# The head of a two-block transformer kernel rebuilt: dummy matmuls, squares on GpSimd, one transfer for small inputs, forget logs earlier, rotary tables later

## The chip, the cores and the metric

The kernel runs on one core of one Trainium2 chip. The metric is device microseconds from start to end of one execution; the profile's page and trace come from one profiled execution of the same program. TensorE is called PE below, VectorE DVE, ScalarE ACT, GpSimd POOL, SyncE SP.

## The reference, cut to what matters

256 tokens of width 1024 pass through two blocks of two layers each. The change touches the start of the first layer, and the place where the second block's rotary tables are made. With the shapes cut out:

```python
def rms_norm(x, g):
    y = x * lax.rsqrt(jnp.mean(x * x, axis=-1, keepdims=True) + NORM_EPS)
    return y * g

def even_layer(x, ln_g, w_in, w_out, ...):
    z = rms_norm(x, ln_g) @ w_in
    aq, ak, av, ag, bq, bk, bv, bg, bf = split_cols(z, EVEN_SPLITS)
    aq, ak = rms_norm(aq, a_qn_g), rms_norm(ak, a_kn_g)      # per head
    lam = exp(sum(a_lq1 * a_lk1)) - exp(sum(a_lq2 * a_lk2)) + lam_init
    a_out = diff_attention(aq, ak, av, lam, lam_init, a_subln_g)   # softmax - lam * softmax
    log_f = jax.nn.log_sigmoid(bf + b_f_bias)
    b_out = forgetting_attention(bq, bk, bv, log_f)          # scores + cumsum of log_f
    mixed = concat([a_out * silu(ag), b_out * silu(bg)])
    return x + mixed @ w_out

def rope_angles(positions, rot_dim):                         # used in the second block alone
    ang = positions[..., None] * ROPE_THETA ** (-arange(0, rot_dim, 2) / rot_dim)
    return cos(ang), sin(ang)
```

## The kernel before, in words

**Matmuls.** All weights lie in one array in the order in which they are used, and come in blocks of 128x1024 (`fetch`, L127, on SP's queue; `raw`). Each operand is split into a high part, which ACT writes by a copy to a rounded type (`wh`, L176, and for activations `ar`, L290), and the rest, which DVE gets by a subtraction (`wl`, L177, and `ar`, L291). Three matmuls (high by high, low by high, high by low) then stand for one. `tokens` (L200) puts tokens on the output's rows, `features` (L231) puts output columns there. A block of weights is split in two pieces of 512 columns.

**The norm of x.** The layer's input is not normalized before the matmul. The factor of each token is worked out beside it and applied to the results. For that ACT squares the four pieces of x (L323, L326), DVE adds them up (L327, `acc`) and folds the two halves (L332), PE sums over the partitions (`col_sums`, L338), and DVE makes the reciprocal square root in nine small operations (L356 and L110 to L120) and puts it into `rk` (L361).

**The head.** In program order: loads of the gains, of x in four pieces and of the first weights; the split of x; the first two projections (`first`, 96 matmuls); the sum of squares; then attention A's queries and keys, whose normalized heads (`u`, L447) are turned by PE with transposes (L399, into `tp`) before scores can be made. The forget gate is eight columns wide (`narrow`, 16 matmuls at L148): its zero padded weights `wn` are cleared by POOL (L140), filled by ACT (L142) and DVE (L143). Its logarithm needs an Exp and a Ln on ACT (L899, L901), and PE sums it over the tokens with the triangular matrix `upto` (L914), which POOL prepares in `u` (L851 to L855) and DVE casts (L857). POOL also clears 12 halves of the block-diagonal key buffers `kbh` and `kbl` (L389), builds masks (L836 to L843), copies pieces of `ident` (L848, L861), and issues the loads of five small inputs (lams, sinks, forget bias, positions, frequencies).

**Order.** Instructions of each engine stand in an order that a scheduler makes from priorities (program order, shifted by `high_priority`), and each engine works its list off in that order, with waits on the other engines. The layer's units run by a string, `ORDER0`, in which AW are attention A's scores and softmaxes, AT the transposes of its weights (L553), BL the forget log. In the page and the trace a line number can be that of a helper: names of tiles tell which use it is.

## Time and profile before

| | us |
|---|---|
| time, median of 3 runs | 864.96 |
| lowest and highest of the 3 | 863.84, 866.10 |
| the profiled execution, its own time | 868.05 |
| its span in the trace | 866.4 |
| PE busy | 840.8 (97%) |
| DVE, ACT, POOL busy | 670.6, 577.7, 40.7 |

The span is from the first to the last instruction of the core; the profiled execution's own time has 1.65 us around it, and lies 3.09 us above the median of the runs without a profile. The mean granted clock of TensorE is 0.996 of full speed. Times inside the trace are counted from the start of the span.

### The profile page before, as it was taken

The numbers are of one execution on the slowest core, as the hardware profiler recorded it, in microseconds if no ns is written. First come the engines' busy times: TensorE is split into PE (matmuls) and PEld (weight loads), VectorE is DVE, ScalarE is ACT, GpSimd is POOL, SyncE is SP. The second block draws the span as 40 slices with busy tenths as digits, with TensorE's granted clock in tenths as the row PEclk, the third lists the DMA queues.
The fourth block names the chain that finished last, engine by engine and source line by source line (L and its number), as shares of the span: only waits on it lengthen the run. The fifth ranks groups of instructions, "written<-read, shape, count | busy, mean of one in ns | idle before, by whom it ended". The sixth has DMA issues, their size and how long they took to land. (4 is left out here: it accounts for less than half of the span.)

```text
span 866.4 us, 17641 instructions
## 1 busy us (share of the span) xinstructions
PE 840.8 (97%) x6554; PEld 808.7 (93%) x6554; DVE 670.6 (77%) x1799; ACT 577.7 (67%) x1379; POOL 40.7 (5%) x90
## 2 busy tenths in 40 slices
PE   6899999999999999999999999998999999999996
PEld 6899999999999999899999999998999998899986
DVE  6779997889898789988665576678999865557654
ACT  6597985779796576976654455556997665346542
POOL 9100000001000100000000000002000000000000
PEclk9999999999999999999999999999999999999999
DMA  7544344644634632246656656543324565555651
GB/s 263 166 161 139 107 142 158 198 158 143 230 97 160 184 108 91 97 137 184 191 194 190 180 192 194 187 139 104 112 73 157 183 190 180 186 187 184 218 163 48
DMA packets 40677, 138.09 MB, mean 159 GB/s; under 512 B 4960, under 2 KB 7152, under 8 KB 40592
## 3 DMA queue, kind: packets, MB, share of 16 engines
q1 hardware_dynamic: 39456, 134.20, 47.9%
q0 software_dynamic: 848, 2.25, 0.9%
q8 instruction: 51, 0.84, 0.4%
q10 hardware_dynamic: 288, 0.52, 0.2%
q14 instruction: 34, 0.28, 0.1%
HBM read 135.91 MB, written 1.05 MB: 158 GB/s over the span
## 5 line engine op out<-in xcount | busy, mean ns | idle before, releaser
L176 ACT ACTIVATE wh<-raw 128x512 fp32r<-128x512 f32 (+2 forms) x548 | 289.8, 570 | 202.8 <-issue 103.2
L177 DVE TENSOR_TENSOR wl<-raw,wh 128x512 fp32r<-128x512 f32 (+2 forms) x548 | 322.4, 618 | 115.6 <-ACT wh L176 111.9
L231 PE MATMUL mm<-ar,wh 128*128 128x256 f32 (+1 forms) x1664 | 301.0, 281 | 0.5 <-ACT ar L714 0.5
L231 PEld LDWEIGHTS mm<-ar,wh 128*128 128x128 f32 (+1 forms) x1664 | 255.0, 188 | 2.0 <-ACT ar L714 1.3
L200 PE MATMUL mm<-wh,ar 128*128 128x256 f32 (+2 forms) x1168 | 237.4, 299 | 8.1 <-ACT wh L176 6.6
L231 PE MATMUL mm<-ar,wl 128*128 128x256 f32 x832 | 232.8, 281 | 0.0
L200 PEld LDWEIGHTS mm<-wh,ar 128*128 128x128 f32 x1168 | 187.9, 192 | 13.4 <-ACT wh L176 6.7
L200 PE MATMUL mm<-wl,ar 128*128 128x256 f32 (+2 forms) x584 | 173.9, 298 | 1.1 <-DVE wl L177 1.1
L231 PEld LDWEIGHTS mm<-ar,wl 128*128 128x128 f32 x832 | 155.9, 188 | 0.3 <-DVE wl L177 0.2
L200 PEld LDWEIGHTS mm<-wl,ar 128*128 128x128 f32 x584 | 111.7, 191 | 4.3 <-DVE wl L177 1.9
L231 PE MATMUL s<-ar,wh 128*128 128x256 f32 x512 | 90.4, 279 | 0.0
L231 PEld LDWEIGHTS s<-ar,wh 128*128 128x128 f32 x512 | 77.9, 188 | 0.0
L231 PE MATMUL s<-ar,wl 128*128 128x256 f32 x256 | 71.4, 279 | 0.0
L537 ACT ACTIVATE se<-sx,mx 128x256 f32<-128x256 f32 (+1 forms) x128 | 57.2, 452 | 4.8 <-DVE mx L534 4.3
L231 PEld LDWEIGHTS s<-ar,wl 128*128 128x128 f32 x256 | 48.1, 188 | 0.0
L231 PE MATMUL pv<-ar,wh 128*128 128x256 f32 x256 | 45.1, 279 | 0.0
L231 PEld LDWEIGHTS pv<-ar,wh 128*128 128x128 f32 x256 | 39.0, 188 | 0.0
L231 PE MATMUL pv<-ar,wl 128*128 128x256 f32 x128 | 35.7, 279 | 0.0
L557 DVE TENSOR_TENSOR pt<-tp,pt 128x384 fp32r<-128x384 f32 x60 | 32.2, 552 | 3.5 <-ACT pt L556 2.8
L506 PE MATMUL s<-kbh,ar 128*128 128x512 f32 (+1 forms) x112 | 31.2, 355 | 0.5 <-ACT kbh L410 0.4
L556 ACT ACTIVATE pt<-tp 128x384 fp32r<-128x384 f32 x60 | 27.9, 486 | 1.1 <-PE tp L555 0.7
L1217 ACT ACTIVATE ar<-u 128x512 fp32r<-128x512 f32 x32 | 20.3, 633 | 11.7 <-DVE u L1215 11.7
(307 smaller groups left out, 1145.8 us busy)
## 6 DMA issues: line engine op xcount, KB each, us to landing
raw<-in_weights SPq DMA_DIRECT2D x242, 512.0 KB, 3.6
bias<-in_alibi SPq DMA_DIRECT2D x12, 192.0 KB, 2.8
bias<-in_relpos POOLq DMA_DIRECT2D x8, 192.0 KB, 2.8
raw<-in_weights SPq DMA_DIRECT2D x4, 384.0 KB, 2.8
xT<-in_x SPq DMA_DIRECT2D x4, 256.0 KB, 4.8
raw<-in_weights SPq DMA_DIRECT2D x4, 192.0 KB, 2.3
raw<-in_weights SPq DMA_DIRECT2D x2, 256.0 KB, 4.4
ar<-in_final_norm POOLq DMA_DIRECT2D x2, 256.0 KB, 5.2
```

The costliest lines, as they stand in the source:

```text
L176: nc.scalar.activation(hi[:, c:e], raw[:, c:e], AF.Copy)
L177: nc.vector.tensor_tensor(out=lo[:, c:e], in0=raw[:, c:e], in1=hi[:, c:e].bitcast(F32), op=OP.subtract)
L200: nc.tensor.matmul(view[t], lhsT=x[:, s], rhs=w[:, j, :], start=(k + j == 0 and i == 0 and (t == 0 or not one)), stop=(k + j == nkt - 1 an ...
L231: nc.tensor.matmul(acc[:width, m * T:(m + 1) * T], lhsT=w[:, j, m * P:m * P + width], rhs=x, start=(k + j == 0 and i == 0 and m == 0), sto ...
L506: nc.tensor.matmul(o, lhsT=a_[:, gq, qt * P:(qt + 1) * P], rhs=b_[:, gk, 0:n], start=(i == 0), stop=(i == 2 and last))
L537: nc.scalar.activation(e[:, c:c + n], x[:, c:c + n], AF.Exp, bias=m[:, i:i + 1], scale=-1.0, accum_out=z[:, i:i + 1])
L556: nc.scalar.activation(h, p[:, :W], AF.Copy)
L557: nc.vector.tensor_tensor(out=l, in0=p[:, :W], in1=h.bitcast(F32), op=OP.subtract)
L1217: nc.scalar.activation(h, u, AF.Copy)
```

## The change

What it does, part by part:

- **Loads.** The gains lie in front of x in one array `xg`; the first piece of x brings them along (128x576). The second piece of x is issued by ACT's queue, the rest by SP's. The five small inputs come as one array `small` (128x298), loaded once on SP's queue into a temporary, and its first 26 columns once more for the rotary tables.
- **Dummy matmuls.** 18 matmuls of 128x128 on a tile of ones (L282 of the changed kernel) stand ahead of everything on PE.
- **Squares on POOL.** All four squares of x and the three adds are TENSOR_TENSOR instructions of GpSimd on 128x512; DVE keeps the fold of the halves (now L342).
- **POOL's list.** The masks come first; the clearing of `kbh` and `kbl` goes far back; the copies of pieces of `ident` go to DVE; four loads leave its queue.
- **Forget logs.** `narrow`, the log and its split are made before attention A's keys are split and before its values; only the sum over tokens (`forget_sum`) stays as the unit BL, after AW1 instead of after AW0.
- **Rotary tables.** The load that they need moves behind the first layer's work on POOL's queue, and with it the whole computation.

The diff at its core:

```diff
-ORDER0 = ("AW0 BL AW1 BV0 AT0 AQ1 AT1 BQ0 ...
+ORDER0 = ("AW0 AW1 BL BV0 AT0 AQ1 AT1 BQ0 ...
...
-        nc.gpsimd.memset(w.bitcast(F32), 0.0)
+        with self.tc.high_priority(offset=500):
+            nc.gpsimd.memset(w.bitcast(F32), 0.0)
...
+    load_x(0, nc.sync)
+    load_x(1, nc.scalar)
+    N.fetch(flat("even_w_in"), 0, 2, 0, 256)
+    N.fetch(flat("even_w_in"), 2, 2, 0, 256, into=N.fetched[:, 512:])
+    load_x(2, nc.sync)
+    load_x(3, nc.sync)
     warm = keep.tile([P, 1], F32, name="warm")
     nc.scalar.activation(warm, ones2[:, 0:1], AF.Exp)
...
+    with tc.high_priority(offset=2000):
+        one, idle = N.arena(F32)[:, :P], N.ps("tp")
+        nc.vector.memset(one, 1.0)
+        for _ in range(WARM):
+            nc.tensor.matmul(idle[:, :P], lhsT=one, rhs=one, start=True, stop=True)
...
+              with tc.high_priority(offset=-300 - 50 * i):
                 nc.gpsimd.memset(z[rw].rearrange("p n (t e c) -> p (n t) e c", t=2, e=2)[:, :, e, :].bitcast(F32), 0.0)
...
     for dp in range(4):
-        squares(dp, st)
+        squares(dp, st, idle=True)
...
+    small = N.tmp("rx", S_COLS)
+    nc.sync.dma_start(out=small, in_=a["small"])
...
-    diff_qk(0)
-    diff_split(0)
-    diff_v(0)
+    with tc.high_priority(offset=300):
+        diff_qk(0)
...
-    nc.gpsimd.memset(both, 0.0)
+    nc.vector.memset(both, 0.0)
     for c in (0, 32):
-        nc.gpsimd.tensor_copy(both[c:c + 32, :], ident[c:c + 32, c:c + 32])
+        nc.vector.tensor_copy(both[c:c + 32, :], ident[c:c + 32, c:c + 32])
...
-        nc.gpsimd.tensor_copy(mine[c:c + 32, :], ident[c:c + 32, c:c + 8])
+        nc.vector.tensor_copy(mine[c:c + 32, :], ident[c:c + 32, c:c + 8])
...
+        return lf4
+
+    def forget_sum():
+        lf4 = gb["f"]
...
+    gb["f"] = forget_log()
+    diff_v(0)
+    diff_split(0)
     U = {"AQ": diff_qk, "AS": diff_split, "AV": diff_v, "AW": diff_weights, "AT": diff_turn, "AO": diff_out, "AN": diff_norm,
-         "BL": forget_log, "BQ": forget_qk, "BS": forget_split, "BV": forget_v, "BW": forget_weights,
+         "BL": forget_sum, "BQ": forget_qk, "BS": forget_split, "BV": forget_v, "BW": forget_weights,
...
-    pos_i = keep.tile([P, 2], I32, name="pos_i")
-    nc.gpsimd.dma_start(out=pos_i, in_=a["positions_2"].rearrange("b (t p) -> p (b t)", p=P))
+    small = N.tmp("gm", T)
+    nc.gpsimd.dma_start(out=small[:, :S_SINK], in_=a["small"][:, :S_SINK])
     pos = keep.tile([P, 2], F32, name="pos")
-    nc.vector.tensor_copy(pos, pos_i)
+    nc.vector.tensor_copy(pos, small[:, S_POS:S_POS + 2].bitcast(I32))
```

Both kernels have the branch of `squares` that `idle=True` takes; before, nothing called it:

```python
            sq = N.tmp("sq") if dp else state["acc"]
            nc.gpsimd.tensor_tensor(out=sq, in0=xf, in1=xf, op=OP.mult)
            if dp:
                nc.gpsimd.tensor_tensor(out=state["acc"], in0=state["acc"], in1=sq, op=OP.add)
```

Where instructions stand now. POOL's list in the changed kernel from its sixth instruction on (`xg` holds x, L325 are the squares, L327 the adds):

```order
L868 MEMSET cmask 128x384
L872 MEMSET tri 128x384
L275 AFFINE_SELECT ident<-ident 128x128
L325 TENSOR_TENSOR acc_276<-xg 128x512
L325 TENSOR_TENSOR sq_278<-xg 128x512
L325 TENSOR_TENSOR sq_281<-xg 128x512
L327 TENSOR_TENSOR acc_276<-acc_276,sq_278 128x512
L327 TENSOR_TENSOR acc_276<-acc_276,sq_281 128x512
L325 TENSOR_TENSOR sq_284<-xg 128x512
L873 AFFINE_SELECT tri<-tri 128x256
L143 MEMSET wn_390 128x1024
L327 TENSOR_TENSOR acc_276<-acc_276,sq_284 128x512
```

Before, 12 clearings of `kbh` and `kbl` (L389) stood there, and no TENSOR_TENSOR. Those 12 clearings now come after the last add, and ahead of the last pieces of the triangular matrix, here `u_374`. POOL further down in the changed kernel:

```order
L400 MEMSET kbl_145 64x4x128 x2
L400 MEMSET kbh_142 64x4x128
L883 MEMSET u_374 128x512
L400 MEMSET kbh_142 64x4x128
L885 AFFINE_SELECT u_374<-u_374 128x128 x2
L887 MEMSET u_374 128x128
```

DVE before, from the first split of x to the fold of the halves (L332): the adds stand between the splits of x (L291) and of the weights (L177), and wait for ACT's squares.

```order
L291 SCALAR_TENSOR_TENSOR ar_94<-xT,gain,ar_93 128x256 x2
L177 TENSOR_TENSOR wl_131<-raw_78,wh_130 128x512
L327 TENSOR_TENSOR acc_257<-acc_257,sq_259 128x512
L291 SCALAR_TENSOR_TENSOR ar_100<-xT,gain,ar_99 128x256 x2
L291 SCALAR_TENSOR_TENSOR ar_106<-xT,gain,ar_105 128x256 x2
L327 TENSOR_TENSOR acc_257<-acc_257,sq_262 128x512
L177 TENSOR_TENSOR wl_163<-raw_160,wh_162 128x512 x2
L327 TENSOR_TENSOR acc_257<-acc_257,sq_265 128x512
L177 TENSOR_TENSOR wl_196<-raw_193,wh_195 128x512 x2
L177 TENSOR_TENSOR wl_228<-raw_225,wh_227 128x512 x2
L332 TENSOR_TENSOR acc_257<-acc_257 128x256
```

DVE in the changed kernel, from the same place to the first operation on PE's column sums (`st_v`); `rx_315` is the small inputs' tile, `wn_390` the forget gate's weights:

```order
L880 COPY both<-ident 32x32 x2
L180 TENSOR_TENSOR wl_182<-raw_179,wh_181 128x512 x2
L893 COPY mine<-ident 32x8 x4
L180 TENSOR_TENSOR wl_215<-raw_212,wh_214 128x512 x2
L180 TENSOR_TENSOR wl_247<-raw_244,wh_246 128x512 x2
L342 TENSOR_TENSOR acc_276<-acc_276 128x256
L802 TENSOR_SCALAR nsink<-rx_315 128x8
L449 TENSOR_REDUCE ms_332<-sq_335 128x8
L146 TENSOR_TENSOR wn_390<-raw_388,wn_390 128x8x8
L180 TENSOR_TENSOR wl_439<-raw_436,wh_438 128x512 x2
L180 TENSOR_TENSOR wl_471<-raw_468,wh_470 128x512 x2
L366 TENSOR_SCALAR st_v_288<-tp_289 128x2
```

The adds are gone from DVE's list, and the fold of the halves (L342) now waits for POOL's last add, with everything below it behind it. Further down on DVE the cast of `upto` (L889, it waits for POOL's `u_374`) stands ahead of the normalized heads (L458) that PE's transposes wait for, as it did before (L857, there some 30 instructions ahead):

```order
L122 SCALAR_TENSOR_TENSOR rs_y_295<-rs_a_296,rs_y_295 128x2
L889 CAST upto<-u_374 128x512
L116 SCALAR_TENSOR_TENSOR rs_a_346<-rs_y_345,ms_332 128x16
L180 TENSOR_TENSOR wl_687<-raw_684,wh_686 128x512
L122 SCALAR_TENSOR_TENSOR rs_y_345<-rs_a_346,rs_y_345 128x16
L458 TENSOR_TENSOR u_333<-u_333,rs_y_345 128x512
L458 TENSOR_TENSOR u_339<-u_339,rs_y_345 128x512
```

On PE the changed kernel has 96 matmuls, the column sums (L348), the 16 narrow ones (L151), 14 matmuls, two that turn the forget gate's rows (L703), 37 matmuls, and then the first transposes of the heads (L410); before it had 96, the column sums, 48, the 16 narrow ones, one, and the transposes (L399).

## Rows read from the trace of the kernel before

**Rows 1.** The page: busy us, share of the span, instructions of each engine.
```profile
PE 840.8 (97%) x6554; PEld 808.7 (93%) x6554; DVE 670.6 (77%) x1799; ACT 577.7 (67%) x1379; POOL 40.7 (5%) x90
```

**Rows 2.** Windows (start:end, length; busy us and instructions of each engine; clock, DMA).
```profile
0.00:6.56 6.56, 0.00 (x1) 0.00 (x1) 1.56 (x10) 2.97 (x6) 5.56 (x15) 1.00 0.55 170
6.56:21.45 14.89, 14.89 (x96) 14.25 (x97) 13.05 (x24) 11.27 (x23) 14.45 (x26) 1.00 0.84 303
...
29.70:33.43 3.73, 0.02 (x1) 0.00 (x1) 3.73 (x22) 1.09 (x2) 0.00 (x0) 1.00 0.58 213
33.43:48.56 15.13, 13.86 (x96) 13.38 (x97) 12.15 (x41) 10.62 (x27) 0.00 (x0) 0.89 0.35 119
48.56:866.40 817.84, 803.82 (x6295) 773.00 (x6293) 634.65 (x1677) 547.11 (x1313) 17.07 (x40) 1.00 0.49 157
```

**Rows 3.** Waits of PE (us in total, times, longest).
```profile
PE mm L200 <- ACT wh L176: 6.6, 1, 6.6
PE tp L399 <- DVE u L447: 3.9, 2, 3.7
PE tp L914 <- ACT ar L909: 1.3, 1, 1.3
```

**Rows 4.** PE's timeline (start, us, operation, count).
```profile
12.06 0.63 PE L200 MATMUL mm<-wh,ar 128*128 128x256 f32 x2
...
12.70 0.63 PE L200 MATMUL mm<-wh,ar 128*128 128x256 f32 x2
...
13.29 0.40 PE L200 MATMUL mm<-wh,ar 128*128 128x256 f32 x2
...
13.64 0.40 PE L200 MATMUL mm<-wh,ar 128*128 128x256 f32 x2
```

**Rows 5.** PE alone behind its two waits (window, length; busy; clock, DMA).
```profile
33.43:38.00 4.57, 4.57 (x26) 0.63 0.49 160
...
47.63:50.00 2.37, 2.37 (x20) 1.00 0.18 41
```

**Rows 6.** DVE's timeline in the head.
```profile
9.79 1.69 DVE L291 SCALAR_TENSOR_TENSOR ar<-xT,gain,ar 128x256 fp32r<-128x256 f32 x4
...
13.82 2.49 DVE L177 TENSOR_TENSOR wl<-raw,wh 128x512 fp32r<-128x512 f32 x4
16.22 0.41 DVE L332 TENSOR_TENSOR acc<-acc 128x256 f32<-128x256 f32 x1
...
25.05 0.15 DVE L356 TENSOR_SCALAR st_v<-tp 128x2 f32<-128x2 f32 x1
...
32.69 1.28 DVE L447 TENSOR_TENSOR u<-u,rs_y 128x512 f32<-128x512 f32 x2
```

**Rows 7.** POOL's four copies at L861: shortest, median, longest in ns.
```profile
L861 POOL COPY mine<-ident x4: 313/356/5512, 10.0 to 11.2; 32x8 f32<-32x8 f32 x4
```

**Rows 8.** POOL's groups by shape (count, busy us, mean ns).
```profile
L389 POOL MEMSET kbh<- 64x512 f32 x6 | 3.1, 518 | 0.5 <-POOLq L1496 0.3
L140 POOL MEMSET wn<- 128x1024 f32 x2 | 1.9, 952 | 283.9 <-PE pv L231 283.9
L1423 POOL TENSOR_TENSOR o<-o,ar 128x256 f32<-128x256 f32 x2 | 1.5, 732 | 47.8 <-ACT sq L1422 47.8
L853 POOL TENSOR_SCALAR_AFFINE_SELECT u<-u 128x128 f32<-128x128 f32 x2 | 0.6, 316 | 0.1
```

**Rows 9.** DVE beside POOL's L1423, which ran from 854.44 to 855.18.
```profile
854.91 0.29 DVE L114 SCALAR_TENSOR_TENSOR rs_a<-rs_y,fv 128x1 f32<-128x1 f32 x1
...
855.62 0.16 DVE L117 SCALAR_TENSOR_TENSOR rs_a<-rs_y,fv 128x1 f32<-128x1 f32 x1
```

**Rows 10.** ACT's timeline: first work on x, a table load, the last gate.
```profile
5.08 0.91 ACT L290 ACTIVATE ar<-xT,gain 128x256 fp32r<-128x256 f32 x2 [2.78 <-DMA xT<-in_x]
...
47.71 1.28 ACT L537 ACT_TABLE_LOAD   x1
...
143.05 1.16 ACT L176 ACTIVATE wh<-raw 128x512 fp32r<-128x512 f32 x2 [1.12 <-issue]
144.12 0.61 ACT L714 ACTIVATE ar<-u 128x512 fp32r<-128x512 f32 x1
```

More of the change, by code (lines that the diff above doesn't have):

```diff
@@ L251, in forward, with load_x @@
     nc.vector.memset(ones2, 1.0)
+    xg = keep.tile([P, G_PAD + KT * T], F32, name="xg")
+    gain = xg[:, :G_PAD]
+    xT = xg[:, G_PAD:].rearrange("p (k t) -> p k t", t=T)
+    def load_x(dp, queue):
+        c = slice(G_PAD + 2 * dp * T if dp else 0, G_PAD + (2 * dp + 2) * T)
+        queue.dma_start(out=xg[:, c], in_=a["x"][:, c])
+    load_x(0, nc.sync)
[4 more added lines that the diff above has]
+    load_x(3, nc.sync)
     warm = keep.tile([P, 1], F32, name="warm")
     nc.scalar.activation(warm, ones2[:, 0:1], AF.Exp)
-    gain = keep.tile([P, 64], F32, name="gain")
-    nc.sync.dma_start(out=gain[:, :G_ROWS], in_=a["gains"])
-    xT = keep.tile([P, KT, T], F32, name="xT")
-    xr = a["x"]
-    def load_x(dp):
-        nc.sync.dma_start(out=xT[:, 2 * dp:2 * dp + 2, :], in_=xr[:, 2 * dp:2 * dp + 2, :])
-    load_x(0)
-    N.fetch(flat("even_w_in"), 0, 2, 0, 256)
-    load_x(1)
-    N.fetch(flat("even_w_in"), 2, 2, 0, 256, into=N.fetched[:, 512:])
-    load_x(2)
-    load_x(3)
     ident = keep.tile([P, P], F32, name="ident")
@@ L771, in forward @@
     nc.vector.tensor_scalar(sub8, gain[:, G_SUB:G_SUB + 1], 0.8, None, op0=OP.mult)
+    small = N.tmp("rx", S_COLS)
+    nc.sync.dma_start(out=small, in_=a["small"])
+    lam4 = small[:, S_LAM:S_COLS].rearrange("p (i f) -> p i f", i=4)
+    ls = N.tiny("ls", 2)
+    lsc = N.tiny("lsc", 64)
+    for i in range(2):
+        nc.vector.scalar_tensor_tensor(out=lsc, in0=lam4[:, 2 * i, :], scalar=1.0, in1=lam4[:, 2 * i + 1, :],
+                                       op0=OP.mult, op1=OP.mult, accum_out=ls[:, i:i + 1])
+    le = N.tiny("le", 2)
+    nc.scalar.activation(le, ls, AF.Exp)
+    nlam = keep.tile([P, 1], F32, name="nlam")
+    nc.vector.scalar_tensor_tensor(out=nlam, in0=le[:, 0:1], scalar=-1.0, in1=le[:, 1:2], op0=OP.mult, op1=OP.add)
+    nc.vector.tensor_scalar(nlam, nlam, -0.2, None, op0=OP.add)
+    sink = keep.tile([P, 8], F32, name="sink")
+    nsink = keep.tile([P, 8], F32, name="nsink")
+    nc.vector.tensor_copy(sink, small[:, S_SINK:S_SINK + 8])
+    nc.vector.tensor_scalar(nsink, small[:, S_SINK:S_SINK + 8], -1.0, None, op0=OP.mult)
+    fbias = keep.tile([P, 8], F32, name="fbias")
+    nc.vector.tensor_copy(fbias, small[:, S_FORGET:S_FORGET + 8])
     U = {}
@@ L1041, in gate @@
         gates(w, (768, 1024, 2816, 3072)[i], R["fm"], osb[i], mixed, 2 * i)
-    pos_i = keep.tile([P, 2], I32, name="pos_i")
-    nc.gpsimd.dma_start(out=pos_i, in_=a["positions_2"].rearrange("b (t p) -> p (b t)", p=P))
+    small = N.tmp("gm", T)
+    nc.gpsimd.dma_start(out=small[:, :S_SINK], in_=a["small"][:, :S_SINK])
     pos = keep.tile([P, 2], F32, name="pos")
-    nc.vector.tensor_copy(pos, pos_i)
-    invf = keep.tile([P, 24], F32, name="invf")
-    nc.gpsimd.dma_start(out=invf, in_=bass.AP(tensor=a["inv_freq"].tensor, offset=a["inv_freq"].offset,
-                                              ap=[[0, P], [1, 24]]))
+    nc.vector.tensor_copy(pos, small[:, S_POS:S_POS + 2].bitcast(I32))
+    invf = small[:, S_FREQ:S_SINK]
     NA = 24
```

43 lines of the change are left out of this document (13 added, 30 removed).

## The prediction, as put on record before the changed kernel ran

> **What bounds the kernel now.** The page comes first: PE is busy 97% of the span [rows 1], so a gain can only come from the 25.6 us in which it is not, or from a faster PE. The windows put nearly half of that in the head: PE does nothing until 6.56, is busy without a gap to 29.70, stands still to 33.43, and has another 1.27 idle by 48.56; behind 48.56 it loses 14.0 in 817.8 us [rows 2]. The waits name the three: the first weights' high parts (6.6), the normalized heads `u` (3.7) and the forget logs' split (1.3) [rows 3]. PE's timeline shows a fourth loss inside busy time: three matmuls take 0.64 us at first (12.06 to 12.70) and 0.35 from 13.29 on [rows 4], half the clock against the full one; and behind the wait for `u` the clock is 0.63 for 4.57 us, which costs 4.57 x 0.37 = 1.7. Behind the wait of 1.27 it stays at 1.00 [rows 5]. So the question is where the first softmax transposes come (48.56 before). The same 213 matmuls and 16 narrow ones stand ahead of them in both kernels, and from about 126 us on PE's order is the same; what they gain or lose there is the kernel's.
>
> **The change part by part.**
>
> *Loads.* x's first piece is issued behind one other DMA now, and ACT's first work on it starts at 5.08 [rows 10]. One issue earlier, but with the gains in it and a second queue beside it: 4.5 to 5.1, I take 4.8.
>
> *Dummy matmuls.* They fill PE's idle 6.6 us and may save the half clock of the first 30 matmuls, 30 x (0.213 - 0.117) = 2.9 us [rows 4]. But PE then only reaches its next wait earlier: what ends that wait is on DVE. I count 0.
>
> *Squares on GpSimd.* The trace has no POOL TENSOR_TENSOR of 128x512. The nearest is 128x256 at 0.73 [rows 8]: twice that less the 0.1 of a smallest memset is 1.36, less the 0.31 of POOL's smallest copy [rows 7] 1.15, and without a fixed part 1.46. Seven of them at 1.36 are 9.5 us (8.0 to 10.2). Alone that is hidden: 4.8 + 9.5 + the masks' 0.45 + some waiting for x's pieces ends near 16.5, when DVE folds the halves now (16.22 + 0.41) [rows 6]. The question is whether POOL runs beside DVE. Of POOL's four copies at L861 one took 5.51 us instead of 0.31 to 0.36 [rows 7]; it ran from 11.18 to 16.69, and DVE's row of two-input operations ended at 16.63. In the other direction DVE's L114, with both inputs in SBUF, took 0.29 instead of 0.16 and ended at 855.20, as POOL's TENSOR_TENSOR ended at 855.18, while operations with one input passed it [rows 9]. So the two exclude each other when both read SBUF, and the stretch is a serial sum. DVE's share until the fold: 8 splits of x at 0.42 and 8 of the weights at 0.60 [rows 6], with a small product of 0.25 8.4. Then 4.8 + 9.5 + 0.45 + 8.4 + 0.41 = 23.6 for the end of the fold; POOL's three memsets between (0.95 for `wn` [rows 8], two small ones) can run beside DVE, or add up to 1.2. I take 24.3, against 16.63 before.
>
> The Trainium skill, SBUF — State Buffer, section Who interferes with whom, says the same in general: a VectorE instruction with two SBUF inputs contends with a GpSimd instruction that reads SBUF, and whoever issues first holds the shared port pair for the whole instruction. By that rule the two would alternate; by the row of 5.51 GpSimd waited through the whole run of VectorE's instructions. The sum of both is 24.3 either way, but alternating also delays the weights' low parts, the third case below.
>
> *From the fold to the norm's factor.* Behind the fold DVE has one product (0.25), four copies (0.4), a reduction (0.6), two small ones, `wn` (0.15) and four weight splits (2.4) before it reads the column sums: 4.0, so `st_v` at 28.3 instead of 25.05 [rows 6]. There the old list had waited for two DMAs; that wait goes with the loads on POOL's queue, and 3.2 us of lateness come in its stead.
>
> *POOL's tail.* Behind its last add (23.9) POOL has the clearings that were moved back: 12 of `kbh` and `kbl` at 0.555 apart (6.7) [rows 8], an affine select (0.3), memsets for the forget logs, `fq` and `fk` (0.59 + 0.65), two of `pt` (0.34), then `u`'s memset and selects (0.54 + 0.59 + 0.2): 9.9, so `upto`'s source is ready at 33.8. DVE comes to that cast after four more weight splits, a reduction and 14 small ones, 28.3 + 4.4 = 32.7, and waits 1.1. Behind the cast stand 12 small operations (1.0), two weight splits (1.2) and the first head (0.6): 33.8 + 0.4 + 2.8 = 37.0 for the transposes, 33.43 before: **+3.6**. PE has its 16 narrow and 51 matmuls meanwhile; with `wn` at about 26 they end by 34.5 at full clock.
>
> *Behind the transposes.* Before, 15.13 us lay between them and the softmax transposes [rows 2]. Three things come off. The forget logs' wait, 1.27: the logs are made ahead of the values, and BL's matmuls stand later. Of the matmuls some 0.6 us moved ahead of the transposes. And the 1.7 of half clock [rows 5]: in my sum PE's long standstill is at 21.5 to 26 instead, and what the clock costs then is paid where PE waits for `u` anyway; its rest before the transposes is 0.8 to 2.5. Bounds 0 and 1.7 (a standstill of 3.7 cost it, one of 1.27 did not); I take 1.7, being nearer the second. That leaves 11.55, and 48.6. Against it stands a new wait: ACT loads its Exp table between the transposes and the first softmax (1.28 each [rows 10]), and two softmaxes are queued where one was: 0 to 2, I take 1.0. First softmax transposes at 49.6, **+1.0**.
>
> *Rotary tables.* Some 20 small DVE operations and one Sin leave the head, where DVE has slack after the transposes; on ACT Sin and two table loads now stand between the layer's third and fourth gate. In the old list the last gate's `ar` waits behind a weight split of ACT until 144.12 [rows 10], so most of the some 2.8 us (two loads and the Sin itself) is taken from slack: 0 to 1.3, I take 0.2. If the slack is gone, 1.3.
>
> *Sum.* 868.05 + 1.0 + 0.2 = 869.2 for the profiled execution, which lay 3.09 above the median; on the median 864.96 + 1.0 = **866.0** with the last term rounded off. This case's own range goes from 863.4 (softmax wait 0, cheap adds) to 868.5 (the half clock stays, wait 2).
>
> **The rivals.**
>
> *No exclusion (faster).* GpSimd's adds run beside DVE, and the last ends by 16.5 to 17. For it: POOL's masks and memsets ran freely at that time, the starved copy is one row, and spans on POOL are rough. Against it: rows 7 and 9 together. Then the fold is done when 96 matmuls are, `st_v` comes by 22, POOL's tail ends at 27, and the transposes come at 28.5 to 29.7, bounded by PE's own 163 matmuls. With 11.55 and the softmax wait of 1 behind them the softmax transposes stand at 41 to 42.3, 6.2 to 7.3 earlier: 864.96 - 6.8 + 0.2 = **858.4**.
>
> *GpSimd takes its turn each time (slower).* Each POOL operation of 1.36 then holds up the next DVE split while PE waits for weights. With all seven in the way, the last low parts come at 22.7 instead of 16, PE starves on and off from 6.4 on, at half clock, and its last 24 matmuls of the 96 take 24 x 0.213 = 5.1 [rows 4]: they end at 27.8. The 67 behind (7.8, the sums and turns 0.9, the half clock's 1.7) end at 38.2, after `u`. The transposes come 1.2 to 1.5 later than in my sum, and the half clock may stay: 867.5 to 869.2, **868.4**. It decides from the point where the last piece of the fourth weight block is split later than 22.
>
> *The head doesn't matter.* The dummies and the earlier load alone would leave the wait for `u` where it is: 865. That lies inside my forecast's range and gets no chance of its own.
>
> **How the numbers follow.** 0.52 for the forecast, 0.32 for no exclusion, 0.16 for the slower case. What a measurement here can tell from no change is about 0.3%, 2.6 us: 862.4 to 867.5. Faster: nearly all of the second case, 0.30, and 0.02 of the first's low end. Slower: 0.12 of the third and 0.10 of the first's upper end. Same: the rest, 0.46. The range runs from 857.5, which keeps two thirds of the faster case, to 869.0, which keeps all but the upper end of the slower one.
>
> **What would show it.** In the changed kernel's trace POOL's L325 and L327 should take about 1.36 each where DVE is idle, and stretch to several us beside DVE's splits, or DVE's L180 and L301 stretch; L342 near 24 (by 17 if there is no exclusion); a wait of PE at the column sums (L348) or the narrow matmuls (L151) of 3 to 5 us; the heads' transposes (L410) near 37, ended by `u`, with DVE's cast of `upto` (L889) waiting for POOL; no wait at the forget sum (L926); the clock at 1.00 behind the transposes; the dummies at L282 up to 6 to 8. I am wrong if the adds end by 17, if POOL's 128x512 costs far from 1.15 to 1.46, or if PE loses time behind 126 us that it did not lose before.

## The result, and the profile after

The changed kernel is slower: 872.44 us, median of 5 runs (872.29 to 874.23), against 864.96 for the kernel before, run beside it (5 runs, 863.84 to 869.40). The ratio is 1.0075, with a 95% interval of 1.0055 to 1.0096. The profiled execution took 872.29 with a span of 870.2; the one of before took 868.05 with 866.4. So the two traces differ by 3.8 us in the span, and the medians by 7.5: the profile of before shows one of its longer executions.

The page after, the part with busy time, share and instructions of each engine, answers to [rows 1]:

```profile
PE 846.0 (97%) x6590; PEld 813.0 (93%) x6590; DVE 678.1 (78%) x1805; ACT 577.1 (66%) x1375; POOL 38.9 (4%) x86
```

PE has 5.1 us more busy time. The dummies alone are 6.7 of it (36 records, two for each of the 18), mostly in what was idle, and the first real matmul starts at 7.6 instead of 6.56; PE's other work took 1.6 us less than before. Where the 3.8 us arise is read from two sets of windows whose bounds are the same instructions in both kernels: the first transposes of the heads, of the first and of the second softmax, a product of attention weights and values (L587, now L598), the column sums of the next layer, the end. Before (columns as in [rows 2]; one row stands there already):

```profile
0.00:33.43 33.43, 23.16 (x165) 22.33 (x166) 23.84 (x84) 19.97 (x40) 23.59 (x50) 1.00 0.72 244
...
48.56:60.27 11.71, 11.71 (x102) 11.71 (x101) 8.27 (x30) 11.56 (x28) 0.00 (x0) 1.00 0.45 153
60.27:133.47 73.20, 72.77 (x582) 70.30 (x581) 67.88 (x227) 61.67 (x155) 0.38 (x2) 1.00 0.40 136
133.47:174.29 40.82, 40.76 (x344) 40.41 (x343) 32.01 (x67) 26.07 (x62) 1.13 (x4) 1.00 0.54 181
174.29:866.40 692.11, 678.58 (x5274) 650.58 (x5272) 526.50 (x1354) 447.81 (x1069) 15.55 (x34) 1.00 0.49 157
```

After:

```profile
0.00:36.06 36.06, 29.84 (x208) 28.52 (x208) 30.50 (x84) 18.92 (x37) 21.11 (x45) 0.95 0.65 228
36.06:49.21 13.15, 11.77 (x91) 11.11 (x91) 10.27 (x34) 11.91 (x33) 0.00 (x0) 1.00 0.40 135
49.21:62.33 13.12, 11.96 (x100) 11.76 (x100) 10.08 (x22) 10.36 (x22) 0.00 (x0) 1.00 0.50 173
62.33:135.89 73.56, 72.82 (x582) 70.34 (x581) 67.71 (x236) 59.05 (x151) 1.11 (x3) 1.00 0.38 128
135.89:177.71 41.82, 40.96 (x345) 40.43 (x344) 33.08 (x78) 28.90 (x65) 1.19 (x4) 1.00 0.52 177
177.71:870.20 692.49, 678.61 (x5274) 650.87 (x5272) 526.49 (x1354) 447.97 (x1069) 15.51 (x34) 1.00 0.49 157
```

Stage by stage: +2.63 to the heads' transposes, -1.98 to the first softmax transposes, +1.41 to the second, +0.36, +1.00 in the stage with the last gate, +0.38 in the rest; 3.80 together. The waits of PE (total, times, longest) name the new losses:

```profile
PE mm L203 <- DVE wl L180: 4.9, 4, 2.0
...
PE mm L234 <- ACT ar L725: 1.3, 2, 0.8
...
PE tp L565 <- DVE se L839: 1.2, 1, 1.2
...
PE tp L564 <- DVE se L839: 0.5, 1, 0.5
...
PE tp L410 <- DVE u L458: 0.3, 2, 0.2
```

The first is new in size: 3.7 of its 4.9 us, in three places, lie before 26 us, where PE waits for low parts of the first weights. Why they are late stands in the timelines of DVE and POOL (start, duration, operation, count). DVE:

```profile
4.66 2.10 DVE L778 SCALAR_TENSOR_TENSOR hg<-xg 128x1 f32<-128x1 f32 x4 [3.40 <-DMA xg<-in_x]
...
8.32 1.75 DVE L180 TENSOR_TENSOR wl<-raw,wh 128x512 fp32r<-128x512 f32 x1
9.99 1.50 DVE L301 SCALAR_TENSOR_TENSOR ar<-xg,ar 128x256 fp32r<-128x256 f32 x1
11.41 1.52 DVE L180 TENSOR_TENSOR wl<-raw,wh 128x512 fp32r<-128x512 f32 x1
...
16.57 3.15 DVE L893 COPY mine<-ident 32x8 f32<-32x8 f32 x4
...
21.11 1.29 DVE L180 TENSOR_TENSOR wl<-raw,wh 128x512 fp32r<-128x512 f32 x2
22.31 0.42 DVE L342 TENSOR_TENSOR acc<-acc 128x256 f32<-128x256 f32 x1
...
26.87 0.15 DVE L366 TENSOR_SCALAR st_v<-tp 128x2 f32<-128x2 f32 x1
```

POOL at the same time:

```profile
4.71 1.04 POOL L325 TENSOR_TENSOR acc<-xg 128x512 f32<-128x512 f32 x1 [2.81 <-DMA xg<-in_x]
5.71 1.04 POOL L325 TENSOR_TENSOR sq<-xg 128x512 f32<-128x512 f32 x1
6.94 1.18 POOL L325 TENSOR_TENSOR sq<-xg 128x512 f32<-128x512 f32 x1 [0.20 <-DMA xg<-in_x]
8.08 1.45 POOL L327 TENSOR_TENSOR acc<-acc,sq 128x512 f32<-128x512 f32 x1
...
9.65 1.56 POOL L327 TENSOR_TENSOR acc<-acc,sq 128x512 f32<-128x512 f32 x1
11.17 1.22 POOL L325 TENSOR_TENSOR sq<-xg 128x512 f32<-128x512 f32 x1
...
17.65 1.29 POOL L327 TENSOR_TENSOR acc<-acc,sq 128x512 f32<-128x512 f32 x1
```

POOL's seven operations take 1.04 to 1.56, 8.8 us in all. DVE's stretch instead: four products with one element per partition take 2.10 and end at 6.76, as POOL's second square does at 6.75; the split that starts at 8.32 ends at 10.07, and its own work is 0.69 elsewhere. POOL's add beside it ended at 9.53, so 0.54 of it lie behind the add. A DVE operation starts, finds POOL reading, and waits until POOL is done. In e12 below, without POOL's arithmetic, the same four rows take 0.37, 0.69, 0.48 and 0.68. The other way in which the squares could make DVE late, by the fold that has to wait for POOL's last add, did not occur: that add ended at 18.94, and the fold (L342) started at 22.31, right behind a split.

### The profile page after: what moved, and what is told of

Read it like the earlier page. It is cut to its first block, busy times and chain, and to the rows that moved or that the text cites. A ratio compares the mean times of both kernels' runs of the same rounds, so it can differ in the third digit from the quotient of the medians.

```text
span 870.2 us, 17724 instructions
## 1 busy us (share of the span) xinstructions
PE 846.0 (97%) x6590; PEld 813.0 (93%) x6590; DVE 678.1 (78%) x1805; ACT 577.1 (66%) x1375; POOL 38.9 (4%) x86
## 3 DMA queue, kind: packets, MB, share of 16 engines
q0 software_dynamic: 704, 2.11, 0.9%
## 4 chain that ended last, share of the span: by engine, by line
PE 78%; DVE 9%; ACT 9%; DMA 2%; issue 2%; SPq 0%; ACTq 0%; DVEq 0%
PE mm L234 31%; PE mm L203 16%; PE s L234 10%; PE pv L234 5%; PE s L203 3%; DVE wl L180 3%; ACT se L548 2%; PE s L517 2%; DMA raw<-in_weights 2%; ACT wh L179 2%; PE pv L203 1%; PE pv L598 1%; ACT pt L567 1%; PE pv L617 1%; PE s L529 1%
## 5 line engine op out<-in xcount | busy, mean ns | idle before, releaser
L203 PE MATMUL mm<-wh,ar 128*128 128x256 f32 (+2 forms) x1168 | 234.8, 297 | 2.1 <-DVE rs_a L119 1.4
L203 PEld LDWEIGHTS mm<-wh,ar 128*128 128x128 f32 x1168 | 185.9, 190 | 7.5 <-issue 1.7
L548 ACT ACTIVATE se<-sx,mx 128x128 f32<-128x128 f32 (+1 forms) x128 | 57.1, 450 | 5.7 <-DVE mx L545 5.2
```

The source lines that it names most:

```text
L203: nc.tensor.matmul(view[t], lhsT=x[:, s], rhs=w[:, j, :], start=(k + j == 0 and i == 0 and (t == 0 or not one)), stop=(k + j == nkt - 1 an ...
L548: nc.scalar.activation(e[:, c:c + n], x[:, c:c + n], AF.Exp, bias=m[:, i:i + 1], scale=-1.0, accum_out=z[:, i:i + 1])
```

## Experiments

Two theories stood against each other. **Exclusion:** GpSimd's arithmetic holds up DVE, and that is the loss. **Order:** the loss is in the moved forget logs and tables, and the squares only shift waits. The runs were taken in four series (e1 to e4, e5 to e8, e9 to e12, e13 to e16), each with executions of before among them. "Span" is that of the profile; before's row gives its median in each series. How far medians can be told apart is shown by e4, which is the kernel before once more: its median lies 1.6 us below that of the 23 other executions of the same kernel in its series.

| run | median (lowest to highest, runs) | ratio to before (95%) | span |
|---|---|---|---|
| before, series 1 / 2 / 3 / 4 | 867.70 / 867.71 / 866.29 / 866.45 (23, 35, 29, 21) | | |
| e1_squares_back | 868.53 (866.71 to 869.53, 12) | 1.0015 (1.0003 to 1.0028) | 865.5 |
| e2_tables_early | 871.78 (870.60 to 873.04, 6) | 1.0055 (1.0038 to 1.0072) | 871.3 |
| e3_forget_back | 873.70 (872.91 to 874.02, 5) | 1.0074 (1.0057 to 1.0091) | 871.2 |
| e4_before_again | 866.08 (864.44 to 868.34, 12) | 0.9990 (0.9977 to 1.0003) | 865.9 |
| e5_write_only | 868.68 (866.26 to 870.64, 10) | 1.0009 (0.9994 to 1.0024) | 865.2 |
| e6_squares_alone | 870.30 (868.17 to 871.18, 12) | 1.0032 (1.0019 to 1.0045) | 868.7 |
| e7_tables_late | 869.42 (867.54 to 870.69, 12) | 1.0022 (1.0008 to 1.0036) | 866.1 |
| e8_exp_ahead | 868.13 (866.92 to 870.46, 12) | 1.0012 (0.9998 to 1.0025) | 867.1 |
| e9_tables_mid | 866.74 (865.36 to 868.93, 12) | 1.0000 (0.9989 to 1.0012) | 867.2 |
| e10_no_dummies | 865.23 (864.69 to 866.35, 12) | 0.9992 (0.9982 to 1.0003) | 863.4 |
| e11_dummies_alone | 866.39 (864.50 to 867.93, 12) | 0.9997 (0.9984 to 1.0010) | 864.3 |
| e12_mid_forget_back | 863.06 (862.91 to 863.19, 6) | 0.9959 (0.9946 to 0.9972) | 861.1 |
| e13_best_no_dummies | 863.45 (862.97 to 864.56, 9) | 0.9960 (0.9946 to 0.9975) | 861.4 |
| e14_best_squares_pool | 871.84 (871.07 to 872.83, 7) | 1.0050 (1.0032 to 1.0068) | 871.1 |
| e15_one_transfer | 864.70 (864.04 to 865.14, 12) | 0.9967 (0.9954 to 0.9980) | 863.4 |
| e16_after_again | 872.49 (871.59 to 874.06, 6) | 1.0060 (1.0040 to 1.0079) | 870.5 |

### The squares: e1, e6, e5

e1 is the changed kernel with the squares on ACT and the adds on DVE again:

```diff
-        squares(dp, st, idle=True)
+        squares(dp, st)
```

> The changed kernel with the squares of x on ACT and their adds on DVE again; all else stays. If the exclusion between GpSimd and DVE is the cause: DVE's splits of x and of the weights take their 0.42 to 0.69 again (1.5 to 1.75 in the changed kernel), the four small products of the gains take about 0.4 instead of 2.1, the 96 first matmuls end near 20 instead of 26, the heads' transposes come at 29 to 31 instead of 36.1, and the first softmax transposes at 42.5 to 45 instead of 49.2. The later losses (gate, softmax waits) stay: 866 to 868, 4 to 6 us below the changed kernel. If the order of the forget logs and the softmax chain is the cause: the heads' transposes come earlier but the softmax transposes stay at 48 to 49, and the time at 871 to 873.

e1 is 3.9 us below the changed kernel (872.44 - 868.53), and PE's column sums start at 20.07 instead of 26.04. That is just outside the 4 to 6 that were expected, and it is no faster than before. What takes the place of the squares is in its waits of PE:

```profile
PE mm L151 <- DVE st_v L366: 2.2, 1, 2.2
PE tp L565 <- DVE se L839: 1.5, 1, 1.5
...
PE mm L234 <- ACT ar L725: 1.3, 2, 0.8
```

The narrow matmuls of the forget gate, the second softmax transposes and the last gate: all places that the moved forget logs and tables made. The first two are gone in e12, where the logs are back; the wait at the gate is gone where the tables are elsewhere (e2, e7, e9).

e6 puts the squares on GpSimd in the kernel before:

```diff
-        squares(dp, st)
+        squares(dp, st, idle=True)
```

> The kernel before with only the squares and their adds on GpSimd. If the exclusion is the cause of the loss: DVE loses 6 to 8 us between 5 and 16 us to GpSimd's seven operations, the 96 first matmuls end at 24 to 26 instead of 21.5, the heads' transposes come 3 to 5 us later than 33.4, and the kernel is 3 to 5 us slower than before, 869 to 871. If the squares hurt only together with the new places of other operations: within 1 of before.

It costs 2.6 us in the median (870.30 against 867.71), a little less than the 3 to 5 expected. POOL's clearings of `kbh` and `kbl` stand ahead of the squares there, so the first square starts at 7.87. DVE's row of splits shows the stretch, 4.50 where [rows 6] have 1.69:

```profile
10.57 4.50 DVE L291 SCALAR_TENSOR_TENSOR ar<-xT,gain,ar 128x256 fp32r<-128x256 f32 x4
```

The column sums come at 28.09 instead of 20.95 in a new profile of before (e4), 7.1 later, and the end 2.8 later: the wait for `u` of 3.6 to 3.7, which both profiles of before have, is gone in e6, so that much of the lateness found cover.

e5 keeps POOL busy but without reading: each of the seven operations becomes four memsets of 128x512, so the sum of squares is left out.

```diff
-            nc.gpsimd.tensor_tensor(out=sq, in0=xf, in1=xf, op=OP.mult)
+            for _ in range(4):
+                nc.gpsimd.memset(sq, 1.0)
```

> The changed kernel with each of GpSimd's seven squares and adds replaced by four memsets of the same 128x512 (0.53 each, so GpSimd is busy longer than before, but reads nothing); the sum of squares is left out. If GpSimd's reading is what holds DVE up: DVE's two-input splits beside the memsets take their 0.42 to 0.69, the gains' small products 0.4, the 96 first matmuls end at 20 to 21, and the time falls like that of the run with the squares back, 866 to 869. If any busy GpSimd holds DVE up: the splits stretch to 1 us and more beside the memsets, and the 96 matmuls end at 25 or later, 872 to 874.

It is level with e1 (868.68), but the time settles little: POOL's queue stood still from 4.9 to 10.0 us, behind the clearing of `wn` that waits for PE, so all splits of x (5.11 to 9.70) ran beside an idle POOL. The rows decide. DVE's operations with two inputs run beside memsets at full speed; copies with one input don't:

```profile
4.57 0.37 DVE L780 SCALAR_TENSOR_TENSOR hg<-xg 128x1 f32<-128x1 f32 x4 [3.31 <-DMA xg<-in_x]
...
11.53 1.95 DVE L895 COPY mine<-ident 32x8 f32<-32x8 f32 x4
13.51 1.29 DVE L180 TENSOR_TENSOR wl<-raw,wh 128x512 fp32r<-128x512 f32 x2
14.72 0.22 DVE L793 SCALAR_TENSOR_TENSOR lsc<-rx 128x64 f32<-128x64 f32 x1
```

From 11.43 to 14.9 POOL ran memsets without a gap. So what stops DVE's two-input operations is that GpSimd reads, not that it works.

### The forget logs: e3

The old order in the changed kernel, with the whole log in the unit BL behind AW0:

```diff
-ORDER0 = ("AW0 AW1 BL BV0 AT0 AQ1 AT1 BQ0 ...
+ORDER0 = ("AW0 BL AW1 BV0 AT0 AQ1 AT1 BQ0 ...
...
-    with tc.high_priority(offset=300):
-        diff_qk(0)
+    diff_qk(0)
+    diff_split(0)
+    diff_v(0)
```

> The changed kernel with the forget logs as one unit again behind the first softmax, in the old order of units and without the raised priority of the queries. If the order is what costs in 49 to 60 us (PE waits 0.5 and 1.2 for the scaled softmax there; the offset grows from 0.6 to 2.05): the old wait of 1.3 for the logs comes back, these two waits go, and the time falls by 0.5 to 2, 870.5 to 872. If the exclusion in the head is the cause of it all: within 0.7 of the changed kernel, 871.8 to 873.

873.70 against 872.44 and 872.49: no gain, and a loss of 1.2 to 1.3 from other series, with ranges that overlap; the ratios to before (1.0074 against 1.0075 and 1.0060) show no clear difference. The trace shows a trade. The heads' transposes come 1.4 earlier (34.64), and the waits at L564 and L565 are gone, but the wait for the logs' split is back with 2.7 us, not the 1.3 that before has, and the first softmax transposes come 2.3 later (51.48). Under the late squares the order of the logs is worth nothing. That it is worth something without them shows below.

### The tables: e2, e7, e8, e9

e2 gives the tables' load a buffer of its own, so that it no longer waits for the first layer's `gm`, and the scheduler moves the tables' work into the head.

```diff
-    small = N.tmp("gm", T)
-    nc.gpsimd.dma_start(out=small[:, :S_SINK], in_=a["small"][:, :S_SINK])
+    small = keep.tile([P, S_SINK], F32, name="small2")
+    nc.gpsimd.dma_start(out=small, in_=a["small"][:, :S_SINK])
```

> The changed kernel with the rotary tables' inputs in a tile of their own, so that tables are made early again (Sin behind the first softmaxes instead of between the third and fourth gate). If the Sin and its two table loads at the gate cost what the trace shows there (0.8 us wait of PE at the last gate, offset to the kernel before 2.4 ahead of it and 3.4 behind it): 1.0 us less, 871.0 to 871.8, no wait for the last gate's operand. If the small DVE operations of the tables were in the way in the head: no gain, 872 to 873.5.

The wait at the gate goes (0.5 is left, behind 180 us, where before has it too), but the heads' transposes come at 40.09 instead of 36.06; PE waits 2.7 us there for the turned rows of the forget gate (L703), 0.7 in the changed kernel. The profiled execution was the slowest of the six (873.04), so these times may not be those of the others. 871.78 in the median is 0.7 less than the changed kernel: no gain that can be told. e7 is e1 with the load into `acc`, which comes free later, behind the layer:

```diff
-    small = N.tmp("gm", T)
+    small = N.tmp("acc")
```

> The changed kernel with the squares back on ACT and DVE, and the rotary tables behind the first layer's output (their inputs come into the buffer of the sum of squares, which is free only there), so that no table load stands between the gates. If the loads at the last gate cost 0.8 to 1.4: no wait of PE at the last gate, 1.0 to 1.4 below the run with the squares back, 866.5 to 867.5; that is 0 to 1 below the kernel before in the same run. If the loads only move to another place where they hurt: 868 to 869.

The gate's wait goes again (0.4), but 1.7 us are lost later: against e4 the same instructions come 1.64 earlier at 174 us and 0.03 later at 226. With 869.42 it lies above both ranges expected, and 0.9 above e1 by the medians. e8 adds to e7 a small Exp behind the Ln, to load the table for the softmax ahead.

```diff
+        nc.scalar.activation(warm, ll[:, 0:1], AF.Exp)
```

> The run before this one, and a tiny Exp on ACT right behind the forget logs' Ln, so that the Exp table is loaded there and not in front of the first softmax. If that load (1.28 us, at 39.1 to 40.4 in the run with the squares back) is what PE waits for at the second softmax transpose (1.5 us): the wait goes to 0 to 0.4, and 1.0 to 1.4 come off, 865 to 866. If DVE's list is what holds the softmax up: no gain, within 0.4 of the run before, or a loss where the load now delays weight splits ahead of the heads' transposes.

The wait at L565 falls from 1.5 to 0.5, the transposes come 1.3 later (33.33): 868.13, not to be told from e1 or e7, where 865 to 866 was expected. e9 is e1 with the tables as a unit of the order behind AT1, about where before had them, and with their load in a buffer of the softmax (`sx`).

```diff
-ORDER0 = ("AW0 AW1 BL BV0 AT0 AQ1 AT1 BQ0 ...
+ORDER0 = ("AW0 AW1 BL BV0 AT0 AQ1 AT1 TB BQ0 ...
```

> The changed kernel with the squares back on ACT and DVE, and the rotary tables as a unit of the first layer behind AT1, near where the kernel before has its Sin (56 us), with their inputs in a buffer of the softmax. If the tables cost only where a table load stands ahead of something that PE waits for: no wait at the last gate and none in the second layer, 1.2 to 1.5 below the run with the squares back, 866.8 to 867.5, and the lead of 2 us over before that this run has at 60 us lasts to the end. If that lead is lost to whatever comes next in any case: 868 to 869, as with the tables late.

866.74, level with before; against e1 that is 1.3 less by the ratios and 1.8 by the medians, from two series and with intervals that overlap. What is firm is the wait at the gate (0.8), which is gone (0.5 left, as in e2). Its profiled execution was the slowest of its twelve (868.93), so its span says little; the place of its loss is plain, though. PE's timeline and ACT's:

```profile
23.78 3.75 PE L151 MATMUL mm<-ar,wn 128*128 128x256 f32 x16 [3.08 <-ACT wh L179]
```

```profile
20.39 1.15 ACT L179 ACTIVATE wh<-raw 128x512 fp32r<-128x512 f32 x2 [3.37 <-PE mm L203]
```

ACT's next weight split waits 3.37 for PE. The narrow weights `wn` are taken from the same set of buffers as `wh` (L141: the same tag), which would explain it; a buffer of their own was not tried. DVE's split waits for ACT, `wn`'s low part stands behind it on DVE, and PE waits for that, with half the clock behind the wait (granted clock 0.50 from 23.78 to 27.53, 16 matmuls in 3.75; 1.00 and 2.11 in e1, where the wait was 2.24).

### The best version and its parts: e12, e13, e14, e10, e11, e15

e12 is e9 with the forget logs in their old place, by the edit of e3. What is left of the change is the loads, POOL's new list, the dummies.

```diff
-ORDER0 = ("AW0 AW1 BL BV0 AT0 AQ1 AT1 TB BQ0 ...
+ORDER0 = ("AW0 BL AW1 BV0 AT0 AQ1 AT1 TB BQ0 ...
```

> The run with the tables in the middle, with the forget logs as one unit behind the first softmax again and the old order of units: what is left of the change are the loads, the dummies and the order of GpSimd's list. If the forget logs' new place is what brings the lead of 2 us at 60 us: that lead is gone, the wait of 1.3 for the logs is back, and the time is 1.5 to 2.5 above the run with the tables in the middle. If the earlier loads bring it: the lead stays, within 0.7.

863.06: 0.41% below before (0.28 to 0.54), and 9.4 below the changed kernel. Neither expected case came: one had the logs' old place cost 1.5 to 2.5, the other put it within 0.7. Here the old place of the forget logs is worth 3.7 (866.74 - 863.06, one series), which e3 could not show. The old wait of 1.3 for the logs is back (L927), and the waits at L151 and L565 are gone. PE's operations into `tp` (count, shortest, median, longest ns, first and last start):

```profile
L410 PE MATMUL tp<-ident,u x8: 272/273/329, 28.5 to 29.6; 128*128 128x128 f32 x8
L348 PE MATMUL tp<-ones,acc x4: 166/251/251, 20.1 to 20.4; 128*128 128x2 f32 x4
...
L564 PE MATMUL tp<-ident,se x2: 271/272/272, 43.1 to 52.6; 128*128 128x128 f32 x2
```

The heads' transposes come 4.9 earlier than in the first profile of before, 4.3 earlier than in the second (e4). e14 is e12 with one edit, the squares on GpSimd:

```diff
-        squares(dp, st)
+        squares(dp, st, idle=True)
```

> The same best run with the squares and adds on GpSimd again and nothing else. If the exclusion is what the changed kernel loses by, whatever stands around it: DVE's splits stretch between 5 and 14 us, the column sums come at 25 to 26 instead of 20, the heads' transposes at 34 to 36 instead of 28.5, and the time is 4 to 7 above, 867 to 870. If the forget logs' place was the larger part of the loss: 1 to 3 above.

871.84, **8.4 more than e13**, which ran beside it, and 8.8 more than e12 (7.9 by the ratios), where 4 to 7 was expected; nearly the changed kernel's time again. The same view, and DVE beside POOL:

```profile
L410 PE MATMUL tp<-ident,u x8: 272/273/329, 35.6 to 36.6; 128*128 128x128 f32 x8
L348 PE MATMUL tp<-ones,acc x4: 166/251/251, 27.4 to 27.6; 128*128 128x2 f32 x4
...
L564 PE MATMUL tp<-ident,se x1: 305/305/305, 51.6 to 51.6; 128*128 128x128 f32 x1
```

```profile
4.60 2.10 DVE L778 SCALAR_TENSOR_TENSOR hg<-xg 128x1 f32<-128x1 f32 x4 [3.34 <-DMA xg<-in_x]
...
12.02 4.03 DVE L301 SCALAR_TENSOR_TENSOR ar<-xg,ar 128x256 fp32r<-128x256 f32 x5
```

The column sums are 7.3 later, the heads' transposes 7.1, the softmax transposes 8.5, the span 10.0 (the profiled execution was the slowest of e14's seven). So some 7 us of the price lie in the head. The next 1.4 are in the wait for the logs' split, in e12 and in e14:

```profile
PE tp L927 <- ACT ar L918: 1.3, 1, 1.3
```

```profile
PE tp L927 <- ACT ar L918: 2.7, 1, 2.7
```

In e6 the wait for `u` covered a part.

The dummies: e10 is e9 without them, e13 is e12 without them, e11 is before with 16 of them.

```diff
-    with tc.high_priority(offset=2000):
-        one, idle = N.arena(F32)[:, :P], N.ps("tp")
-        nc.vector.memset(one, 1.0)
-        for _ in range(WARM):
-            nc.tensor.matmul(idle[:, :P], lhsT=one, rhs=one, start=True, stop=True)
```

> The run before this one without the 18 dummy matmuls. If they are hidden behind the wait for the column sums and for DVE, as forecast: the first 96 matmuls begin and run at half clock up to 13 us and end 1.5 to 3 later, but the heads' transposes come within 0.5, and the time within 0.7. If the head is now bound by PE: the heads' transposes and the time are 1 to 3 us later.

> The kernel before with 16 dummy matmuls at its start and nothing else. If what PE wins is lost at its next wait: the first matmuls come 0.1 to 0.3 apart from the start, the 96 end near 18.5 to 19.5 instead of 21, PE waits 2 us more for the heads, and the time stays within 0.7 of before. If the half clock of the start reaches the end: 1.5 to 2.9 less, 0.2 to 0.3%.

> The run with the tables in the middle and the old place of the forget logs (863.06, 0.41% below before), without its dummies. If the dummies are worth nothing: within 0.7, 862.4 to 863.8. If they hurt also here (they cost 1.5 in the run with the forget logs ahead): 861.5 to 862.3. If they carry part of its lead, since PE no longer waits behind them: 864.5 to 866.

863.45 without against 863.06 with, from two series; 866.39 with against 866.29 without: nothing that can be told. In e9 they cost: e10 is 1.5 below it in one series, with 10 of its 12 executions below 866.0 and 11 of e9's above, where 0.7 at most was expected. Why was not tried. They do raise the speed of the first matmuls. In e11 three take 0.35 from 7.99 on, before 0.64 [rows 4]; PE then waits for the next weights, and the column sums start at 21.4, within 0.5 of both profiles of before, where 18.5 to 19.5 was expected:

```profile
7.99 0.28 PE L201 MATMUL mm<-wl,ar 128*128 128x256 f32 x1
8.11 0.40 PE L201 MATMUL mm<-wh,ar 128*128 128x256 f32 x2
8.35 0.28 PE L201 MATMUL mm<-wl,ar 128*128 128x256 f32 x1
...
12.27 0.50 PE L201 MATMUL mm<-wh,ar 128*128 128x256 f32 x2 [1.01 <-ACT wh L177]
```

e15 is before with the five small inputs in one transfer on SP's queue:

```diff
+    small = keep.tile([P, S_COLS], F32, name="small")
+    nc.sync.dma_start(out=small, in_=a["small"])
...
-    nc.gpsimd.dma_start(out=nsink, in_=bass.AP(tensor=a["c_sinks"].tensor, offset=a["c_sinks"].offset,
-                                               ap=[[0, P], [1, 8]]))
```

> The kernel before with only the small inputs in one transfer on SP's queue. If the two waits of DVE for the lams and the sinks (1.1 and 2.4 us ahead of the norm's factor) are what the best run has won: the factor's first operation comes 2 to 3.5 earlier than 25, the heads' transposes at 29.5 to 31, and the time is 2 to 3.5 below before, 0.2 to 0.4%. If the rotary tables, whose inputs are now there early and whose small operations move ahead of the factor, eat it: within 1 of before. If the win comes from x's earlier landing: within 0.7.

864.70, 0.33% below before (0.20 to 0.46), where 0.2 to 0.4% was expected. `st_v` comes at 23.21 instead of 25.05 [rows 6], the heads' transposes at 30.59 instead of 33.43. By the ratios that is four fifths of e12's gain.

### Both kernels again: e4, e16

> The kernel before itself, as a control: ratio 1.000 within 0.3%, and a second profile of it. If the profiled execution of before that the forecast was made from was a slow one of it, this one's span lies near 863 instead of 866.4, and the trace shows where the 3 us lie; if they lie around the span, the span is 866 again and the time 865.

> The changed kernel itself on the chip of these runs, for their differences to it, and a second profile: 872 to 874, 0.55 to 0.95% above before; the heads' transposes at 35.5 to 37.

The changed kernel repeats within 0.05 us in the median. Before does not: its executions spread from 863.7 to 870.3, with medians of 866.3 to 867.7 in the four series. In e4's profile the heads' transposes come at 32.77, 0.66 before those of the first profile, and that difference stays to the end. What makes it vary was not found; e12's six runs spread by 0.3 us. The second pair of profiles (e16 less e4) has the changed kernel 4.05 us behind at the heads' transposes, 2.00 at the first softmax transposes (49.97 against 47.97), 3.42 at the second and 4.6 at the end; the first pair had 2.63, 0.65, 2.06 and 3.8. The medians of series 4 differ by 6.0. So the traces hold 3.8 and 4.6 of a difference of 6.0 to 7.5 between medians: the profiled executions of before were slow ones among theirs (868.05 against a median of 864.96, 867.60 against 866.08), and no trace shows one of its fast ones.

## Why the prediction was wrong, and where it was right

The predicted case, same within 0.3%, did not come; the slower one did, and beyond the range (869.0). The forecast of 866.0 misses 872.44 by 6.4: 3.1 of it in the base from which it starts, 1.4 at the second softmax transposes and 0.8 at the last gate; smaller terms make up the rest.

**Right: the exclusion, and its size in the head.** The sum of DVE and POOL gave 24.3 for the end of the fold, which came at 22.73; `st_v` 28.3 against 26.87; the heads' transposes 37.0 against 36.06; the first softmax transposes +1.0 against +0.65 in this pair of profiles and +2.00 in the other. POOL's operations took 1.04 to 1.56 against 1.36 (1.15 to 1.46), 8.8 in all against 9.5. "No exclusion", with its 0.32, is out: e14 and e6 show the stretch and its price. The Trainium skill, SBUF — State Buffer, section Who interferes with whom, says that a VectorE instruction with two SBUF inputs contends with a GpSimd one that reads SBUF, not with one that only writes, and describes the shared port pair as an exclusive lock. These traces agree: 2.10 instead of 0.37 beside TENSOR_TENSOR, 1.29 for two splits beside memsets in e5, and a split that ended 0.54 behind POOL's add, with work of its own of 0.69.

**Wrong in the forecast's picture: who waits.** That the heads' transposes came within 1 us of the forecast is in part luck: it had them wait for `u` behind POOL's tail and the cast of `upto`, which held nothing up; PE, late from inside the 96, came within 0.2 us of `u`. The forecast let GpSimd be starved, as its copy of 5.51 us was [rows 7], and put PE's standstill behind the 96 matmuls. GpSimd had its turn each time, as the third case said: PE starved inside the 96 (three waits of 3.7 us for low parts, one of 0.6 for x's), did not wait at the column sums, and waited 0.2 for `u` at the transposes. The clock followed that starving (columns as in [rows 2], clock 0.52):

```profile
13.00:16.50 3.50, 3.50 (x16) 3.38 (x17) 3.46 (x9) 0.00 (x0) 0.20 (x1) 0.52 0.04 9
```

The third case put the end of the 96 at 27.8 and the transposes at 38.2; they came at 26.04 and 36.06. A part of that reads from POOL's row: the last add stood behind `wn`'s clearing, which waited for PE until 16.73, so that only six operations met the splits. POOL's tail was early, too: `upto`'s source was complete at 28.09, not 33.8, and DVE's cast, at 31.84, did not wait. So the third case had the mechanism, and an amount that was 2 us too high.

**Failed step 1: the working stopped at the first softmax transposes.** It counted 1.0, of 0 to 2, for two queued softmaxes and the Exp table, took that for all, and carried the offset from there unchanged to the end. PE waited there 0.5, then 1.2 for the second one of these softmaxes (L565), and the stage behind 49.21 has 13.12 us for 11.71: 1.41 that no term held. The two waits together are 1.7, so the term was too small and ended too early. e12, with the logs in the old place, has no wait at L565; e8, with the Exp table loaded ahead, has 0.5 there instead of 1.5.

**Failed step 2: the last gate.** I took 0.2 of 0 to 1.3, reading slack from one row of ACT [rows 10]. The stage takes 1.00 more, PE waits 0.8 for `ar`, and two table loads stand on ACT, that did not stand there before:

```profile
138.37 1.28 ACT L1086 ACT_TABLE_LOAD   x1
...
143.85 1.28 ACT L743 ACT_TABLE_LOAD   x1
```

The wait is gone in e2, e7 and e9, where the tables lie elsewhere, though only e9 came out lower for it, and that not firmly. A value near the high end of the bound was the one to take. The prediction had named a loss behind 126 us as a sign of being wrong.

**Failed step 3: the base.** The sum for the profiled execution was 869.25 before rounding; it took 872.29. These 3.04 are the two steps above (1.41 and 0.8), 0.74 in the later stages, 0.44 outside the span, less the 0.35 by which the head was better. Then 3.09 were taken off for the distance of before's profile from its median. The changed kernel has no such distance (872.29 and 872.44), and before's median came out at 866.3 to 867.7 in the later series. With before's middle taken there, 1.3 to 2.8 of the 6.4 missing us disappear. One kernel's spread had been treated as a constant of both.

**Right: the dummies at 0** (e11, e13; in e9 they cost 1.5), for the reason given: PE reaches its next wait earlier. **And the clock:** it is 1.00 behind the transposes, where [rows 5] had 0.63, while the stretch before them has 0.95 in place of 1.00. The half clock of before's first matmuls, though, was read from their durations alone: the clock column of [rows 2] has 1.00 there. The changed kernel's three matmuls in 0.64 from 14.12 on stand where the column has 0.52.

**A slip that moved nothing:** in "no exclusion", 48.56 less 41 is 7.5, not 7.3.

**What the forecast did not separate.** Both theories hold in part, and the edits hide one another. The one transfer gains 1.8 us by the medians of its series and 2.9 by the ratio (e15); the squares cost 2.6 in before (e6) and 8.4 to 8.8 in the best version (e14); the forget logs cost nothing under the squares (e3) and 3.7 without them (e9 to e12); the tables cost about 1 at the gate, which taking them away did not firmly give back (e7, e9). A sum of single effects is not the effect of the sum: whoever removes the largest wait sees the next.

## What to carry to other kernels

Arithmetic on GpSimd is not spare capacity while VectorE splits or adds pairs of SBUF tiles: here each split waited for the operation beside it, and where little else covered it (e14) the price was 8.4 to 8.8 us for seven operations that took 9.1. Clearing tiles there did not hold up such operations (e5), but it did hold up VectorE's copies. When a change bundles edits, take each alone and each away from the whole; here the squares lost time alone, the logs lost it once the squares were undone, and the one part shown to gain, a single transfer for small inputs, was worth 0.33% alone. And measure the spread of the kernel before, before you take an offset from it.
